# New costs in the pass that orders a transformer block's instructions: column operands, plain float32 products, result delays and load lead

## The chip, the cores and the metric

The kernel runs on one core of one Trainium2 chip. The core has a matrix engine (TensorE, PE in the profile), a vector engine (VectorE, DVE), a scalar engine (ScalarE, ACT), a general engine (GpSimd, POOL) and a queue engine (SyncE, SP) that issues nearly all DMA transfers. The metric is device time in microseconds (us) of one execution; the median of several runs is compared.

## The reference

One layer of an encoder on x of 2048 tokens by 1024 features, float32, then a last RMSNorm:

```
xn = RMSNorm(x)
aq ak av mq mk mv mo i f ga gm = split(xn @ w_in)
A = attention: own chunk of 64 and 8 chunks before, clipped relative bias, 8 heads of 64
M = mLSTM over chunks, 4 heads of 128; mq and mk pass a causal convolution of width 4 and silu;
    headwise RMSNorm, times sigmoid(mo)
y = sigmoid(ga) * (A @ w_att_proj) + sigmoid(gm) * (M @ w_mlstm_proj)
x = x + y @ w_out
x = x + relu(RMSNorm(x) @ w_up)^2 @ w_down          # w_up: 1024 x 4096
```

## The kernel before, in words

**Number format.** Each float32 operand of a large product is split into two parts, the rounded value and the rest (both of type float32r). One product is three matrix products: high by high, high by low, low by high. For a weight tile of 128x1024, ACT writes the high part (line 614) and DVE the low part (line 616) in `split_now`; for an activation tile of 128x512, lines 1324 or 1326 on ACT and 1329 or 1331 on DVE do the same in `split`. Some smaller products stay plain float32: in the recurrence (`rec_head`, lines 1786, 1800, 1801, 1802) and in sums over features.

**Stages.** The tokens are four blocks of 512. Blocks 0 and 1 are projected block by block (matmul lines 697 to 699, `mm3`), with attention and recurrence of these blocks running between. Then come products in `quad` (line 782), which forms a 2x2 block product from seven products of sums, so DVE has sums of operands and of results to make: operand sums in `take_rest` (line 1897) and `take_parts` (lines 1924, 1936), copies and sums of results in `combine` (line 1959 on ACT, line 1967 on DVE). The order is: gates and output projection of blocks 0 and 1; the projections of blocks 2 and 3 (the names in `IN_ORDER`, among them `mq` and `mk`, which go through `conv_far` with lines 2129 to 2142, and last `mo`, with lines 2100 and 2106 in `after_in`); the up and down products of blocks 0 and 1; recurrence and attention of blocks 2 and 3 between the down products; then output projection, up and down of blocks 2 and 3.

**Memory.** Nearly everything that lives long goes to DRAM and comes back: SP issues stores (line 2220) and loads (for instance 578 and 573 for weights, 1917 for inputs of the up product). Tiles come from small pools: 3 split weight tiles `wsp`, 4 raw weight tiles `wraw`, 16 tiles `ctx`, 6 `tmp`, 28 split operands `r`, 8 accumulation banks.

**What sets the order.** Two passes do. `Flow` (line 97) runs the generators and fixes the program order and which tile each step gets; the change leaves it alone. `Order` (line 226) then takes that program, finds which instruction must follow which (`graph`), and writes a fixed order for each engine, and for SP's queue, by a forward walk (`run`, line 338). Three methods feed the walk. `cost` gives each instruction a duration. `lag` gives the time from one instruction's end to the start of one that needs it. `due` gives each instruction the latest start that does not hold up the matrix products, worked back from their planned times; an SP transfer is taken there to need its own cost and `FAR` more. In the walk an engine takes, of the instructions that are ready, the one with the earliest due time; PE takes the one that is earliest in program order. When a transfer lands in the walk depends on `REACH`, `LAND` and its size, not on `FAR`.

```
for j in self.succ[k]:
    to = self.eng[j]
    r = end + self.lag(k, j)
    at[j] = max(at[j], r)
    safe[j] = max(safe[j], r + (self.MARGIN[e] if to != "PE" and (to != e or e == "SP") else 0.0))
    left[j] -= 1
    if not left[j]:
        heapq.heappush(soon[to], (safe[j], due[j], j))
```

At run time each engine goes through its list in order, and an instruction that waits holds all that stand behind it.

Of the kernel before, what the change touches and what calls it, by code (L numbers as in the profile page):

```python
# [24 lines left out]
F32 = mybir.dt.float32  # L25
# [200 lines left out]
class Order:  # L226
# [1 line left out]

    MARGIN = dict(PE=600.0, Activation=100.0, DVE=100.0, Pool=100.0, SP=2500.0)
    WAKE = dict(PE=43.0, DVE=23.0, Activation=23.0, Pool=69.0, SP=16.0)  # L230
    REACH, LAND, FAR, FLY = 1400.0, 1100.0, 2500.0, 8

    def __init__(self, tc):
        self.tc = tc
# [33 lines left out]
    def cost(self, i, e):  # L268
        ins, outs = self.operands(i.ins), self.operands(i.outs)
        n = max(self.count(a) for a in ins + outs)  # L270
        bank = any(a.tensor.name.startswith("bank") for a in ins + outs)
        if e == "PE":
            return max(110.0, 13.7 + self.count(outs[0]) / 2.4)
        if e == "SP":
            return 365.0
        if e == "Activation":
            return (75 if bank else 93) + 0.84 * n + (190 if len(outs) > 1 else 0)
        if e == "Pool":
            return 1200.0 if n <= 8 else 80 + 1.27 * n
        if n <= 4:  # L280
            return 155.0
        two = sum(self.count(a) > 4 for a in ins) > 1
        return 60 + (1.13 if two or bank else 0.66) * n + (80 if len(outs) > 1 else 0)

    def transfer(self, i):
        a, b = self.operands((i.outs[0], i.ins[0]))
# [29 lines left out]
    def lag(self, j, k):  # L316
        e, to = self.eng[j], self.eng[k]
        if e == to != "SP":
            return 0.0
        t = self.WAKE[to] + (0.0 if e == "SP" else 13.0)  # L320
        return t + (0.0 if e != "PE" else 175.0 if self.dur[j] >= 140.0 else 130.0)

    def due(self):
# [55 lines left out]
class Layer:  # L379
    LATE, LATE_SPLIT = 3000.0, 2500.0  # L380
# [2333 lines left out]
```

## Time and profile before

| | |
|---|---|
| median of 3 runs | 2759.5 us (2759.44, 2759.5, 2763.28) |
| the profiled execution | 2762.9 us, its span 2761.1 us |
| PE busy | 2748.6 us, 13054 matmuls |
| DVE busy | 2060.5 us |
| ACT busy | 1490.9 us |
| granted TensorE clock, mean | 0.999 |
| DMA | 678.64 MB, 246 GB/s |

The span is the time from the first to the last instruction; the profiled execution took 1.8 us more than its span. The busy time of PE counts matmuls that overlap in the pipeline, so PE can be busy by the profile and still issue matmuls later than it could. The time from one matmul's start to the next one's shows that better.

### The profile page before, as it was taken

What the parts mean: (1) busy time and instruction counts of PE and PEld (TensorE: products, weight loads), DVE (VectorE), ACT (ScalarE), POOL (GpSimd) and SP (SyncE); (2) the same over time, 40 slices, a digit from 0 to 9 for tenths busy, and PEclk for the clock granted to TensorE, in tenths of its full rate; (3) what the DMA queues carried; (4) which work ended last, traced back from release to release, by engine and by line L of the source; (5) the groups of instructions that cost most, each with busy time, mean ns of one, the idle gap of its engine ahead of it and who ended that gap; (6) DMA issues with size and microseconds to landing.
All of it is one profiled execution on the core that took longest, in us unless ns stands there. A gap on an engine that the chain in (4) does not pass through costs nothing.

```text
span 2761.1 us, 38681 instructions
## 1 busy us (share of the span) xinstructions
PE 2748.6 (100%) x13054; PEld 2291.3 (83%) x13054; DVE 2060.5 (75%) x3793; ACT 1490.9 (54%) x2617; POOL 49.9 (2%) x101
## 2 busy tenths in 40 slices
PE   9999999999999999999999999999999999999999
PEld 7888888888878888778888888888888888888888
DVE  7796799668996866876676788889888656555566
ACT  5664576534454545575556566566335655554444
POOL 0010001000000000000000000000000000000000
PEclk9999999999999999999999999999999999999999
DMA  7968859768866587588888978868977667676664
GB/s 283 292 220 263 235 161 305 252 199 309 279 200 228 195 285 251 170 262 311 298 288 283 303 242 253 251 203 255 293 232 262 209 218 262 237 247 215 197 222 163
DMA packets 329190, 678.64 MB, mean 246 GB/s; under 512 B 36856, under 2 KB 67744, under 8 KB 328992
## 3 DMA queue, kind: packets, MB, share of 16 engines
q1 hardware_dynamic: 328848, 676.17, 74.4%
q8 instruction: 102, 1.67, 0.3%
q14 instruction: 96, 0.79, 0.1%
q10 hardware_dynamic: 144, 0.01, 0.0%
HBM read 472.59 MB, written 203.44 MB: 245 GB/s over the span
## 4 chain that ended last, share of the span: by engine, by line
PE 95%; DVE 2%; ACT 1%; issue 1%; DMA 0%; SPq 0%; DVEq 0%; ACTq 0%
PE bank L782 42%; PE bank L697 13%; PE bank L699 13%; PE bank L698 13%; PE bank L811 3%; PE bank L1515 2%; PE bank L1488 2%; PE bank L1546 2%; PE bank L1802 1%; PE bank L1801 1%; DVE ctx L2138 1%; PE bank L1800 1%; PE bank L1786 0%; DVE wsp L616 0%; PE bank L862 0%
## 5 line engine op out<-in xcount | busy, mean ns | idle before, releaser
L782 PE MATMUL bank<-r,wsp 128*128 128x512 f32 x5544 | 1266.6, 391 | 5.4 <-ACT r L1324 2.0
L782 PEld LDWEIGHTS bank<-r,wsp 128*128 128x128 f32 x5544 | 1040.5, 188 | 223.7 <-ACT r L1324 2.5
L616 DVE TENSOR_TENSOR wsp<-wraw,wsp 128x1024 fp32r<-128x1024 f32 x458 | 560.2, 1223 | 371.1 <-ACT wsp L614 360.6
L614 ACT CAST wsp<-wraw 128x1024 fp32r<-128x1024 f32 x458 | 481.3, 1051 | 545.9 <-PE bank L698 224.4
L697 PE MATMUL bank<-r,wsp 128*128 128x512 f32 x1456 | 580.7, 399 | 0.5 <-ACT ctx L1779 0.5
L699 PE MATMUL bank<-r,wsp 128*128 128x512 f32 x1456 | 569.7, 391 | 0.0
L698 PE MATMUL bank<-r,wsp 128*128 128x512 f32 x1456 | 569.1, 391 | 0.0
L699 PEld LDWEIGHTS bank<-r,wsp 128*128 128x128 f32 x1456 | 273.6, 188 | 58.0
L697 PEld LDWEIGHTS bank<-r,wsp 128*128 128x128 f32 x1456 | 274.0, 188 | 50.9 <-ACT ctx L1779 0.9
L698 PEld LDWEIGHTS bank<-r,wsp 128*128 128x128 f32 x1456 | 274.3, 188 | 49.5
L1967 DVE TENSOR_TENSOR ctx<-bank,ctx 128x512 f32<-128x512 f32 x186 | 127.3, 688 | 103.5 <-PE bank L782 103.0
L1329 DVE TENSOR_TENSOR r<-r 128x512 fp32r<-128x512 f32 x248 | 163.4, 687 | 13.0 <-ACT r L1324 12.4
L1324 ACT CAST r<-r 128x512 fp32r<-128x512 f32 x248 | 147.5, 621 | 21.8 <-DMA r<-u 20.0
L1959 ACT COPY ctx<-bank 128x512 f32<-128x512 f32 x186 | 107.9, 581 | 81.8 <-PE bank L782 70.1
L1530 ACT ACTIVATE sc<-sc,scs 128x640 f32<-128x640 f32 (+4 forms) x128 | 97.5, 763 | 75.6 <-DVE scs L1527 69.9
L1551 DVE TENSOR_TENSOR r<-bank,r 128x512 fp32r<-128x512 f32 (+1 forms) x168 | 97.2, 597 | 20.1 <-ACT r L1549 19.1
L1549 ACT CAST r<-bank 128x512 fp32r<-128x512 f32 (+1 forms) x168 | 82.5, 518 | 51.5 <-PE bank L1546 50.0
L1521 DVE CUSTOM_DVE_ANT_0 sc<-bank,bias 128x320 f32<-128x320 f32 (+3 forms) x240 | 103.8, 463 | 3.6 <-PE bank L1515 2.8
L2298 ACT ACTIVATE ctx<-ctx 128x512 f32<-128x512 f32 x96 | 60.5, 630 | 84.8 <-DVE ctx L1967 84.7
L1488 PE MATMUL bank<-r,r 128*128 128x512 f32 x336 | 94.7, 363 | 0.0
L633 DVE TENSOR_TENSOR wraw<-wraw,wraw 128x1024 f32<-128x1024 f32 x76 | 92.8, 1223 | 1.8
L1515 PE MATMUL bank<-r,r 128*128 128x320 f32 (+3 forms) x480 | 85.7, 305 | 0.0
(269 smaller groups left out, 2738.1 us busy)
## 6 DMA issues: line engine op xcount, KB each, us to landing
wraw<-in_wf SPq DMA_DIRECT2D x178, 512.0 KB, 4.6
wraw<-wsum SPq DMA_DIRECT2D x136, 512.0 KB, 4.4
r<-u SPq DMA_DIRECT2D x224, 256.0 KB, 4.3
wraw<-in_w SPq DMA_DIRECT2D x87, 512.0 KB, 5.0
u<-ctx SPq DMA_DIRECT2D x128, 256.0 KB, 2.4
ctx<-in_wf SPq DMA_DIRECT2D x112, 256.0 KB, 4.6
wsum<-ctx SPq DMA_DIRECT2D x112, 256.0 KB, 4.5
u<-tmp SPq DMA_DIRECT2D x96, 256.0 KB, 3.7
```

What stands on the lines that cost most here:

```text
L614: nc.scalar.copy(w[:, 0], raw)
L616: nc.vector.tensor_sub(w[:, 1], raw, w[:, 0].bitcast(F32))
L697: mm(ps, lh, rh, start=first, stop=False)
L698: mm(ps, lh, rl, start=False, stop=False)
L699: mm(ps, ll, rh, start=False, stop=last)
L782: mm(ps, wv[:, x, k, n], a[:, y], start=new and k == 0 and x == y == 0, stop=k == 3 and x == 1, skip_group_check=True)
L1324: self.nc.scalar.copy(dst[:, 0], src)
L1329: self.nc.vector.tensor_sub(dst[:, 1], src, dst[:, 0].bitcast(F32))
L1488: nc.tensor.matmul(acc[:, :, c0:c0 + w], st, sl[:, :, o:o + w], start=n == 0, stop=n == total - 1)
L1515: nc.tensor.matmul(bks[x][:, :w], q[:, y, i * P:(i + 1) * P], kf[:, f * P + x * w:f * P + x * w + w], start=y == 0, stop=y == 1)
L1959: nc.scalar.copy(t[:, o:o + 512], ps)
L1967: nc.vector.tensor_add(t[:, o:o + 512], ps, t[:, o:o + 512])
```

## The change

Only `Order` is touched. What is computed, the tiles and the transfers stay as they are; the five lists can come out in another order.

- `cost`, PE: a plain float32 product counts double; transposes don't.
- `cost`, ACT: 92 ns for each input beyond the first (a column of one value per partition as scale or bias), in place of 190 ns for a second output (a sum over the row).
- `cost`, DVE: 62 ns when there are three inputs (a column among them), in place of 80 ns for a second output.
- `lag`: between instructions of one engine, where one needs the other's result, 125 ns (ACT), 85 ns (DVE) or 60 ns (POOL) in place of 0; to another engine, 98 ns more after ACT and 50 ns more after DVE.
- `FAR`: 5000 ns in place of 2500.

```diff
     WAKE = dict(PE=43.0, DVE=23.0, Activation=23.0, Pool=69.0, SP=16.0)
-    REACH, LAND, FAR, FLY = 1400.0, 1100.0, 2500.0, 8
+    AGAIN = dict(PE=0.0, Activation=125.0, DVE=85.0, Pool=60.0)
+    LATE = dict(PE=0.0, Activation=98.0, DVE=50.0, Pool=0.0)
+    REACH, LAND, FAR, FLY = 1400.0, 1100.0, 5000.0, 8
...
         if e == "PE":
-            return max(110.0, 13.7 + self.count(outs[0]) / 2.4)
+            plain = ins[0].dtype == F32 and not i.is_transpose
+            return max(110.0, 13.7 + self.count(outs[0]) / 2.4) * (2.0 if plain else 1.0)
...
         if e == "Activation":
-            return (75 if bank else 93) + 0.84 * n + (190 if len(outs) > 1 else 0)
+            return (75 if bank else 93) + 0.84 * n + 92 * (len(ins) - 1)
...
-        return 60 + (1.13 if two or bank else 0.66) * n + (80 if len(outs) > 1 else 0)
+        return 60 + (1.13 if two or bank else 0.66) * n + (62 if len(ins) > 2 else 0)
...
         if e == to != "SP":
-            return 0.0
-        t = self.WAKE[to] + (0.0 if e == "SP" else 13.0)
+            return self.AGAIN[e]
+        t = self.WAKE[to] + (0.0 if e == "SP" else 13.0 + self.LATE[e])
```

## Prediction

> **What bounds the kernel now.** I read the page first, then PE's waits, then the time from one matmul's start to the next at those waits.
>
> ```profile
> span 2761.1 us, 38681 instructions
> PE 2748.6 (100%) x13054; PEld 2291.3 (83%) x13054; DVE 2060.5 (75%) x3793; ACT 1490.9 (54%) x2617; POOL 49.9 (2%) x101
> PE 95%; DVE 2%; ACT 1%; issue 1%; DMA 0%; SPq 0%; DVEq 0%; ACTq 0%
> ```
>
> PE sets the time: 95% of the chain that ended last is matmuls. The change alters no matmul, so it can only remove PE's waits, add new ones, or change how kinds of matmuls alternate.
>
> ```profile
> PE bank L782 <- ACT r L1324: 2.0, 1, 2.0
> PE bank L782 <- ACT ctx L1959: 2.0, 1, 2.0
> PE bank L782 <- ACT r L1326: 1.1, 1, 1.1
> PE bank L438 <- DVE ones L435: 1.0, 1, 1.0
> PE bank L1645 <- DVE cum L1641: 0.7, 2, 0.3
> PE bank L697 <- ACT ctx L1779: 0.5, 1, 0.5
> PE bank L782 <- DVE r L1329: 0.2, 1, 0.2
> ```
>
> These are all of PE's named waits; L438 is the start, where nothing can be gained. The others are six places with 6.5 us of idle time. Idle time understates them, so here is PE's timeline at the three large ones.
>
> ```profile
> 715.74 1.27 PE L782 MATMUL bank<-r,wsp 128*128 128x512 f32 x4
> 718.14 0.74 PE L782 MATMUL bank<-r,wsp 128*128 128x512 f32 x2 [1.13 <-ACT r L1326]
> ...
> 1145.90 0.84 PE L782 MATMUL bank<-r,wsp 128*128 128x512 f32 x3
> 1148.74 5.30 PE L782 MATMUL bank<-r,wsp 128*128 128x512 f32 x15 [2.00 <-ACT ctx L1959]
> ...
> 1212.40 0.84 PE L782 MATMUL bank<-r,wsp 128*128 128x512 f32 x3
> 1215.28 0.50 PE L782 MATMUL bank<-r,wsp 128*128 128x512 f32 x1 [2.04 <-ACT r L1324]
> 1216.01 0.74 PE L782 MATMUL bank<-r,wsp 128*128 128x512 f32 x2 [0.23 <-DVE r L1329]
> ```
>
> Three undisturbed matmuls take 0.84, one longer than a start-to-start interval: with 0.39 for the last one the interval is (0.84 - 0.39) / 2 = 0.226 us. **C**, at 716: four intervals take 2.40 in place of 0.90, a loss of 1.5. **A**, at 1146: three take 2.84 in place of 0.68, a loss of 2.16; and the 15 matmuls behind it take 5.30 in place of 14 x 0.226 + 0.39 = 3.55, a further 1.75. **B**, at 1212: four take 3.61, a loss of 2.7. The small ones are 0.5 (**D**, L697) and 0.7 (**E**, L1645, two places); with about 0.16 hidden in the pipeline before each (0.39 - 0.226), they come to 0.7 and 1.0. The sum, 1.5 + 3.9 + 2.7 + 0.7 + 1.0 = 9.8 us, is what a perfect order could save.
>
> **What the change does, part by part.** No instruction and no byte is added: PE's 13054, DVE's 3793 and ACT's 2617 instructions and SP's transfers stay, and any of them may move in its list. The question is what the planner misjudged where PE stalled.
>
> ```profile
> 1108.00:1148.00 40.00, 38.74 (x171) 31.76 (x170) 38.26 (x55) 20.80 (x30) 0.00 (x0) 1.00 0.44 147
> L2138 DVE SCALAR_TENSOR_TENSOR ctx<-ctx,cvw,ctx 128x512 f32<-128x512 f32 x21 | 15.6, 749 | 0.6 <-ACT ctx L2131 0.2
> 1105.40 0.76 DVE ctx L2138
> 1106.18 0.75 DVE ctx L2138
> ```
>
> *Column operands and dependent steps, at A.* In the 40 us before A, DVE is busy for 38.26. The largest group is the convolution, 21 steps of L2138, each with a column and mostly needing the one before. The old formula gives 60 + 1.13 x 512 = 639 ns and no delay to the dependent one; the chain of waits has them start 0.78 us apart. The new one gives 639 + 62 + 85 = 786 ns. Over 21 steps the old plan is 21 x 0.14 = 2.9 us short, against a stall of 2.16. So PE's bank was to be emptied (L1967 on DVE, then L1959 on ACT) at a time when DVE was in truth still busy with L2138. With true durations the pass sees the queue and puts L1967 and L1959 ahead where their due times say so. They pass steps of `conv_far`, whose stores then go out later on SP; what is late next are the `ctx` tiles they free, and 16 of those exist.
>
> ```profile
> 1183.00:1214.00 31.00, 30.24 (x134) 24.73 (x132) 22.46 (x32) 24.96 (x39) 0.00 (x0) 1.00 0.84 273
> L2106 ACT ACTIVATE ctx<-ctx,ghead 128x512 f32<-128x512 f32 x8 | 6.5, 817 | 0.2
> L1924 ACT ACTIVATE ctx<-ctx,gcol 128x512 f32<-128x512 f32 x3 | 2.2, 718 | 2.7 <-DMA ctx<-x 2.7
> L1924 ACT ACTIVATE tmp<-tmp,gcol 128x512 f32<-128x512 f32 x3 | 2.1, 713 | 0.0
> 1207.29 0.33 SPq L2220
> 1207.72 6.12 DMA ctx<-x
> ```
>
> *The same at B, and the loads.* Here ACT is full until 1207. Eight L2106 with two columns and six L1924 with one cost the old plan 8 x 184 + 6 x 92 = 2.0 us less than the new one gives them. SP, which issues in order, held the load of x behind the store of the last L2106, and the load landed 6.12 us after its issue. `due` allowed 2.5 us for it.
>
> ```profile
> r<-u SPq DMA_DIRECT2D x224, 256.0 KB, 4.3
> u<-ctx SPq DMA_DIRECT2D x128, 256.0 KB, 2.4
> ```
>
> 5000 ns fits loads like r<-u (4.3 us) and overstates such stores as u<-ctx, at 2.4. In `due` this gives a step 2.5 us more urgency for each transfer between it and PE, 5 us for a store with a load behind it; the chain at B has both.
>
> [...]
>
> *Result delays and sums over a row, in attention.*
>
> ```profile
> L1530 ACT ACTIVATE sc<-sc,scs 128x640 f32<-128x640 f32 x96 | 79.7, 831 | 63.4 <-DVE scs L1527 62.8
> L1530 ACT ACTIVATION_READ_ACCUMULATOR sc<-sc,scs 128x1 f32 x128 | 24.2, 189 | 0.0
> 1540.00:1960.00 420.00, 420.00 (x2273) 360.10 (x2273) 366.19 (x955) 256.69 (x563) 12.96 (x35) 1.00 0.82 251
> ```
>
> Dropping 190 and 80 ns for a second output is wrong taken alone: L1530 still has a second instruction. The old cost of L1530 was 93 + 538 + 190 = 821, the new one 723, with 98 for its delay 821 again. L1521, 320 wide, goes by the formulas from 502 to 422, with 85 for the dependent step behind it 507. So the latencies of the softmax chain come out level or later; only ACT's occupancy is short, 128 x 98 ns = 12.5 us over stages in which ACT is busy for 256.69 of 420 us. PE does not idle there (420.00 of 420.00), since it can pass over an attention step that is not ready. I take nothing; the bound is one stall of D's size (0.7) in each of the two attention stages, 1.4, and no gain, as nothing is lost there now.
>
> *Plain products at double cost.*
>
> ```profile
> 1794.90 0.47 PE L697 MATMUL bank<-r,wsp 128*128 128x512 f32 x1
> 1795.21 0.40 PE L698 MATMUL bank<-r,wsp 128*128 128x512 f32 x1
> 1795.44 0.40 PE L699 MATMUL bank<-r,wsp 128*128 128x512 f32 x1
> 1795.68 0.39 PE L1800 MATMUL bank<-r,ctx 128*128 128x129 f32 x2
> 1795.90 0.39 PE L1801 MATMUL bank<-r,ctx 128*128 128x129 f32 x2
> L1802 PE MATMUL bank<-cst,r 128*128 128x129 f32 x128 | 24.7, 275 | 0.0
> ```
>
> Each plain product is two passes and takes 0.22 us (1795.68 to 1795.90): the new 220 ns is right, the old 110 half. The old plan thus let PE run ahead of the truth, a hidden reserve of 110 ns per product for the engines that feed it; L1802 alone has 64 products, 7 us. The reserve goes, and the added delays take its place: nothing, with the same bound of 1.4. A return from plain to split products costs 0.31 - 0.23 = 0.08 (1794.90 to 1795.21). If every fourth of L1802's 64 groups joined or left another, that is 16 x 0.08 = 1.3 either way; I take 0.
>
> **The sum.** A and B, where the planner's error is the size of the stall: 6.6, of which I take three quarters, 5.0, since DVE and ACT stay full and something else is late next. E hangs on a chain of small dependent steps, which AGAIN now prices: half, 0.5. C and D: nothing; C's work has no column, it is DVE out of time. New stalls in the reshuffled lists: one of C's size, 1.5 (between 0 and the slower rival's price). That is 5.0 + 0.5 - 1.5 = 4.0 off the profiled execution's 2762.9, 2758.9. That execution is 3.4 above the median, two of the three runs lie at 2759.5, and nothing shown says where the 3.4 is spent; I carry the difference over: 2759.5 - 4.0 = **2755.5**. Its own range is 2753 to 2758.5.
>
> [...]
>
> **The rivals.**
> 1. *All stalls go*: the six come from late planning alone and the order is now free of them: 2759.5 - 9.8 = 2749.7. For it: DVE and ACT have time left over the whole span. Against: at C DVE has none for 28 us.
> [...]
> 3. *It doesn't do what it says*: true costs change the lists little, or move a stall for each one removed: 2759.5, give or take 1.5.
> 4. *Slower: the lead starves PE's own chain.* What is stored and loaded again before use now counts as up to 5 us more urgent than what PE waits for directly. With DVE full this decides as soon as a bank's emptying is put off by more than the time until PE needs the bank, 24 matmuls or 5.4 us. At A one more convolution tile ahead of L1967 is 3 x 0.75 + 0.69 = 2.9 and the slow pace behind it 1.75; at C the five L2181, whose results are stored, would go ahead of the operand splits, 5 x 0.6 = 3.0. With no gain elsewhere: 2759.5 + 7.7 = 2767.2.
>
> ```profile
> 690.00:718.00 28.00, 27.01 (x119) 21.74 (x117) 27.74 (x44) 11.85 (x16) 0.00 (x0) 1.00 0.85 293
> L2181 DVE TENSOR_TENSOR ctx<-bank,ctx 128x512 f32<-128x512 f32 x5 | 3.4, 685 | 0.0
> ```
>
> For it: DVE is busy for 27.74 of these 28 us. Against: a `ctx` tile freed by a store is itself what L1959 needs to empty a bank.
>
> **How the numbers follow.** Chances: forecast 0.40; all stalls go 0.17; lead worthless 0.12; no effect 0.12; slower 0.19. A measurement here can tell about 0.2%, 5.5 us, from no change, so faster means below 2754.0 and slower above 2765.0. Faster: 0.17 and a third of the forecast's 0.40, 0.30. Slower: 0.19 and 0.01 of the rest, 0.20. Within: 0.50. The range runs from the first rival to just short of the fourth, 2749.5 to 2766.
>
> **What would show it.** In the changed kernel's PE waits, the rows L782 <- ACT ctx L1959 and L782 <- ACT r L1324 should be gone or under 1 us, the clock near 1150 at 1.00, and the load of x for the up product issued before the last L2106's store. L1645 <- DVE cum should shrink, L1326's row at C stay. [...] The forecast is wrong if waits named above remain and the time falls all the same: then alternation of matmul kinds or another part outside these waits matters.

## The result, and the profile after

The changed kernel's median is 2754.12 us (14 runs, 2752.87 to 2755.94), against 2760.45 us (14 runs, 2758.91 to 2765.14) for the kernel before: 6.3 us less, a ratio of 0.9976 with a 95% interval of 0.9968 to 0.9984. The forecast was 2755.5, 1.4 us above. The prediction had given faster 0.30 and no change 0.50, with a bound of 5.5 us, or 2754.0. By the difference this is just faster; by the time alone, worked from the earlier median of 2759.5, it lies 0.1 on the other side of the bound. The two profiled executions lie further apart, 2762.9 and 2753.5. Why is a point of its own below.

The page of the changed kernel, with the lines that answer to the first three shown of before (line numbers in it are 3 higher, because the change adds lines above):

```profile
span 2751.8 us, 38708 instructions
PE 2745.0 (100%) x13054; PEld 2287.2 (83%) x13054; DVE 2035.7 (74%) x3793; ACT 1491.8 (54%) x2617; POOL 51.1 (2%) x101
PE 99%; DVE 0%; DMA 0%; ACT 0%; SPq 0%; issue 0%; ACTq 0%; DVEq 0%
```

The instruction counts of PE, DVE and ACT are those of before. The chain that ended last is now matmuls for 99% in place of 95%. All of PE's named waits (what waited, on what, us in total, times, longest):

```profile
PE bank L441 <- DVE ones L438: 1.0, 1, 1.0
PE bank L785 <- DVE r L1334: 0.6, 1, 0.6
```

L441 is the start. Of the six places A to E one is left, C, and PE's timeline there and at A reads (start, length, the idle time before it in brackets):

```profile
704.73 10.34 PE L785 MATMUL bank<-r,wsp 128*128 128x512 f32 x43
715.70 2.63 PE L785 MATMUL bank<-r,wsp 128*128 128x512 f32 x10 [0.63 <-DVE r L1334]
...
1142.74 5.60 PE L785 MATMUL bank<-r,wsp 128*128 128x512 f32 x24
```

At C the last of the 43 matmuls starts at 704.73 + 10.34 - 0.39 = 714.68 and the next at 715.70, 1.02 later in place of 0.226: a loss of 0.8. But the 43 have themselves taken 10.34 in place of 42 x 0.227 + 0.39 = 9.92, and the ten behind the wait lose 0.2. In all C loses 1.4 here. Before, the same count over the 140 matmuls around it gives 1.6 (the prediction counted 1.5), so little is gained at C, although the named wait fell from 1.1 to 0.6. The 24 matmuls where A was take 5.60, which is 23 x 0.226 + 0.39: nothing is lost. The same stretches at A and B, each a little earlier than before because less was lost ahead of them (start and end, length, then busy time of PE, its weight loads, DVE, ACT, POOL, then the granted clock, DMA share and GB/s):

```profile
1108.00:1148.00 40.00, 40.00 (x178) 33.11 (x178) 37.60 (x54) 22.08 (x32) 0.00 (x0) 1.00 0.48 156
1183.00:1214.00 31.00, 31.00 (x139) 25.44 (x137) 22.28 (x33) 24.89 (x40) 0.00 (x0) 1.00 0.73 245
```

DVE is still busy for 37.60 of the 40 us at A, and ACT for 24.89 of the 31 at B. The engines that feed PE have no more time than before; their work stands in another order.

**What is different at A.** Before, DVE and ACT worked in turns, and each had put an instruction that waited for the other ahead of what PE needed. DVE's timeline before:

```profile
1146.26 0.69 DVE L2142 SCALAR_TENSOR_TENSOR ctx<-ctx,ctx 128x512 f32<-128x512 f32 x1 [0.76 <-ACT ctx L2140]
1146.86 0.68 DVE L1967 TENSOR_TENSOR ctx<-bank,ctx 128x512 f32<-128x512 f32 x1
```

ACT's timeline before, and then after:

```profile
1147.58 0.63 ACT L2100 ACTIVATE ctx<-ctx 128x512 f32<-128x512 f32 x1 [0.43 <-DVE ctx L1967]
1148.12 0.57 ACT L1959 COPY ctx<-bank 128x512 f32<-128x512 f32 x1
```

```profile
1143.07 0.57 ACT L1962 COPY ctx<-bank 128x512 f32<-128x512 f32 x1
1145.13 1.24 ACT L2103 ACTIVATE ctx<-ctx 128x512 f32<-128x512 f32 x2 [1.50 <-DVE ctx L1970]
```

These are the same copy in both lists, of bank_134 into ctx_121. Before, its row (L1959, 1148.12) names no wait of its own: it stood behind L2100, which waited 0.43 for DVE's L1967, which stood behind L2142, which waited 0.76 for ACT's L2140. PE went on at 1148.74, 0.05 after the copy's end. After, the copy (L1962) stands ahead of the waiting instruction (L2103), and the 1.50 that this one waits costs nothing. (The copy also needs its tile stored and free; whether that held before 1148.12 the rows don't say.)

**What is different at B.** ACT's timeline before, then after, then SP's after:

```profile
1210.10 1.05 ACT L614 CAST wsp<-wraw 128x1024 fp32r<-128x1024 f32 x1 [2.84 <-PE bank L782]
1213.86 0.72 ACT L1924 ACTIVATE ctx<-ctx,gcol 128x512 f32<-128x512 f32 x1 [2.70 <-DMA ctx<-x]
```

```profile
1204.14 1.05 ACT L617 CAST wsp<-wraw 128x1024 fp32r<-128x1024 f32 x1 [3.32 <-PE bank L785]
1207.57 0.73 ACT L1927 ACTIVATE ctx<-ctx,gcol 128x512 f32<-128x512 f32 x1
```

```profile
1200.14 1.02 SPq L2223 DMA_DIRECT2D mfar<-ctx  x2
1201.26 0.43 SPq L1920 DMA_DIRECT2D ctx<-x  x1
```

The weight cast is the same instruction of ACT's list in both, and PE releases it in both, so it serves as a mark: it comes 5.96 us earlier after. The load of x comes 6.46 earlier (1207.72 to 1201.26), so by that mark it gained only 0.5 us, and it still stands behind the last store that L2109 (before: L2106) feeds. The operand is ready 6.3 earlier. PE, which lost 2.7 us here, now loses nothing, because its own list changed. This is the start of the stretch in both lists (index of the matmul: output <- operands; r_88 is the split of the late tile):

```
before  5594 bank_131<-r_79  5595 bank_133<-r_88 (x3)  5598 bank_133<-r_69 (x3)  5601 bank_134<-r_88 (x3)
        5604 bank_134<-r_69 (x3)  5607 bank_131<-r_79 (x2)  5609 bank_131<-r_77 (x3)  5612 bank_131<-r_87 (x3)
after   5594 bank_131<-r_79 (x3)  5597 bank_131<-r_77 (x3)  5600 bank_131<-r_87 (x3)  5603 bank_131<-r_81
        5604 bank_133<-r_88  5605 bank_134<-r_88  5606 bank_131<-r_81  5607 bank_133<-r_88 (x2)
```

The changed walk expects the operand later and gives PE 9 other matmuls first: 9 x 0.226 = 2.0 us, the size of the idle time of before (2.04). These are the rest of bank_131, which before stood behind the late operand. With the delays alone the late operand is first used at place 5603, with the columns alone at 5592, so this move is the delays' work. In all, some 500 places of PE's list hold another matmul than before.

### The profile page after: what moved, and what is told of

Its sections match the earlier page's. It is cut to its first block, busy times and chain, and to the rows that moved or that the text cites. A ratio compares the mean times of both kernels' runs of the same rounds, so it can differ in the third digit from the quotient of the medians.

```text
span 2751.8 us, 38708 instructions
## 1 busy us (share of the span) xinstructions
PE 2745.0 (100%) x13054; PEld 2287.2 (83%) x13054; DVE 2035.7 (74%) x3793; ACT 1491.8 (54%) x2617; POOL 51.1 (2%) x101
## 4 chain that ended last, share of the span: by engine, by line
PE 99%; DVE 0%; DMA 0%; ACT 0%; SPq 0%; issue 0%; ACTq 0%; DVEq 0%
PE bank L785 45%; PE bank L700 13%; PE bank L702 13%; PE bank L701 13%; PE bank L814 3%; PE bank L1518 2%; PE bank L1491 2%; PE bank L1549 2%; PE bank L1804 1%; PE bank L1805 1%; PE bank L1789 1%; PE bank L1803 1%; PE bank L865 0%; PE bank L1592 0%; PE bank L904 0%; PE bank L1778 0%
## 5 line engine op out<-in xcount | busy, mean ns | idle before, releaser
L1962 ACT COPY ctx<-bank 128x512 f32<-128x512 f32 x186 | 107.8, 582 | 91.6 <-PE bank L785 81.2
```

What stands on the lines that cost most here:

```text
L1962: nc.scalar.copy(t[:, o:o + 512], ps)
```

## The experiments

Each is one kernel with a few lines of the ordering pass changed, compared with the kernel before on the same chip. Line numbers in a kernel shift by as many lines as its edit adds. The delays are the two tables `AGAIN` and `LATE`; the plain products are the doubled PE cost; the columns are the ACT and DVE cost lines; the lead is `FAR`. Times are medians; ratios are to the kernel before.

**A nudge.** One constant of the DVE cost of the kernel before is 1 ns larger, which says nothing new of the chip and shuffles the lists.

```diff
-        return 60 + (1.13 if two or bank else 0.66) * n + (80 if len(outs) > 1 else 0)
+        return 61 + (1.13 if two or bank else 0.66) * n + (80 if len(outs) > 1 else 0)
```

> The kernel before with one meaningless number changed: a base cost of 61 ns in place of 60 on DVE. Theory 1 (the pass was wrong about true durations at the stalls): nothing is put right, so A and B stay, PE's waits of 1 us or more keep a sum of 4 to 7 us, ratio 0.9995 to 1.0010. Theory 2 (a redraw: any new order happens to have other stalls, and the order before was an unlucky one): most of the gain appears here too, ratio 0.9975 to 0.9985, and the stalls lie elsewhere.

2759.54 us, ratio 0.9994 (0.9985 to 1.0003), profiled execution 2758.68. PE's waits:

```profile
PE bank L782 <- ACT ctx L1959: 1.7, 1, 1.7
PE bank L782 <- ACT r L1326: 1.1, 1, 1.1
PE bank L782 <- ACT r L1324: 0.8, 1, 0.8
```

PE's timeline at A:

```profile
1139.76 6.51 PE L782 MATMUL bank<-r,wsp 128*128 128x512 f32 x28
1147.95 10.27 PE L782 MATMUL bank<-r,wsp 128*128 128x512 f32 x44 [1.68 <-ACT ctx L1959]
```

A, B and C stall in the same places with the same releasers: a new draw of the lists alone doesn't take them away. Their size moves, though: the waits of 1 us or more come to 2.8 us, where 4 to 7 was expected. A loses 1.9 (1139.76 + 27 x 0.226 = 1145.86 to 1147.95, less 0.226), and no slow pace follows: 44 matmuls in 10.27 are 43 x 0.23 + 0.39. B waits 0.8 in place of 2.0.

**The lead alone**, in the kernel before.

```diff
-    REACH, LAND, FAR, FLY = 1400.0, 1100.0, 2500.0, 8
+    REACH, LAND, FAR, FLY = 1400.0, 1100.0, 5000.0, 8
```

> The kernel before with the lead for loads at 5000 ns alone. Theory 1 with the lead as one of its causes: B goes (the load of x for the up product is issued some us earlier), A and the other waits stay, 2.5 to 3 us, ratio 0.9988 to 0.9992. The slower rival (the lead starves PE's own chain): A grows by 2 us or more and C grows, ratio above 1.0005. Theory 2: like the nudge.

2758.32 us, ratio 0.9988 (0.998 to 0.9997), profiled execution 2757.74. Of its PE waits:

```profile
PE bank L782 <- ACT ctx L1959: 1.3, 1, 1.3
PE bank L1800 <- DMA r<-mvfar: 1.1, 1, 1.1
...
PE bank L782 <- DVE r L1331: 0.2, 1, 0.2
```

B is gone, and here it is the lead that removes it: SP issues the load of x at 1201.76, 6 us earlier, and PE's list uses the late operand 10 matmuls sooner than before (place 5585), without a wait. A shrinks, C's wait is down to 0.2, E stays, and a load of `mvfar` is late that was not. Nothing of the kind that the slower rival named appears: no new stall behind DVE steps whose results are stored.

**The columns alone**, with the second-output terms dropped as in the change, in the kernel before.

```diff
-            return (75 if bank else 93) + 0.84 * n + (190 if len(outs) > 1 else 0)
+            return (75 if bank else 93) + 0.84 * n + 92 * (len(ins) - 1)
...
-        return 60 + (1.13 if two or bank else 0.66) * n + (80 if len(outs) > 1 else 0)
+        return 60 + (1.13 if two or bank else 0.66) * n + (62 if len(ins) > 2 else 0)
```

> The kernel before with the new costs of column operands (ACT 92 ns each, DVE 62 ns) in place of the second-output costs, alone. Theory 1: A shrinks by about half (1.3 of the 2.9 us by which the plan was short there) and B by 2 us of planning, so 2 to 4 us off, ratio 0.9986 to 0.9993. If the dropped second-output cost hurts, new small waits behind the softmax steps, lines 1530 to 1551, 0.3 to 1.4 us. Theory 2: like the nudge.

2757.18 us, ratio 0.9986 (0.9977 to 0.9995), profiled execution 2758.08.

```profile
PE bank L782 <- ACT r L1326: 1.1, 1, 1.1
...
PE bank L1645 <- DVE cum L1641: 0.6, 2, 0.3
PE bank L699 <- DVE r L1282: 0.5, 1, 0.5
```

A and B are gone with the columns alone; C and E stay whole, as steps without a column should. D's row has given way to one of the same size at L699; a fourth wait, of 0.2, is at L1546.

**The delays alone**, in the kernel before.

```diff
+    AGAIN = dict(PE=0.0, Activation=125.0, DVE=85.0, Pool=60.0)
+    LATE = dict(PE=0.0, Activation=98.0, DVE=50.0, Pool=0.0)
...
-            return 0.0
-        t = self.WAKE[to] + (0.0 if e == "SP" else 13.0)
+            return self.AGAIN[e]
+        t = self.WAKE[to] + (0.0 if e == "SP" else 13.0 + self.LATE[e])
```

> The kernel before with the result delays alone (AGAIN within an engine, LATE to another). Theory 1: A shrinks by the other half (1.6 us of planning error is the dependent steps' delay) and the two waits at the gates' running maximum, E, go; B stays unless the delays reach it; 2 to 4 us off, ratio 0.9986 to 0.9993. Theory 2: like the nudge.

2762.96 us, ratio 1.0009 (1.0 to 1.0017), profiled execution 2766.78: no gain. PE's waits:

```profile
PE bank L1225 <- POOL r_far L1257: 3.4, 1, 3.4
PE bank L1802 <- DMA r<-mvfar: 3.3, 1, 3.3
...
PE bank L784 <- DVE r L1333: 0.4, 1, 0.4
```

The load that ends the second, in the chain of waits of that stretch (issued, time to landing):

```profile
442.92 9.99 DMA r<-mvfar
```

PE's timeline behind the first (3.44 us in it), and the stretch there with the columns of above:

```profile
502.12 0.63 PE L700 MATMUL bank<-r,wsp 128*128 128x512 f32 x1
502.55 0.63 PE L701 MATMUL bank<-r,wsp 128*128 128x512 f32 x1
```

```profile
501.80:504.50 2.70, 2.70 (x8) 2.12 (x8) 1.29 (x2) 1.92 (x5) 0.00 (x0) 0.50 0.00 1
```

A, B and E are gone here too, and C (L784) waits 0.4. But two stalls of 3.3 and 3.4 us have come, both in the recurrence and its norm, where PE works on plain products. The walk of this kernel prices those at half (110 ns, where the prediction's rows have 0.22 us), so in it PE arrives there, and everything else is planned, at times that are not the chip's. How much of the two stalls is due to that, and how much to a load and a power that took long in this execution, it doesn't separate. They are hardly this execution's alone: all 11 executions of this kernel have a mean granted clock of 0.999 or less on record. Here it is 0.998, most likely for what lies behind the two stalls: a clock of 0.50 behind the first, and behind the second plain products that start 0.42 to 0.44 us apart in place of 0.22.

**Each part taken back from the changed kernel.** Four kernels, each the changed one without one part: `FAR` at 2500; the plain products at single cost; the old ACT and DVE cost lines; no delays (the diffs above, backwards, and for the plain products this):

```diff
-            return max(110.0, 13.7 + self.count(outs[0]) / 2.4) * (2.0 if plain else 1.0)
+            return max(110.0, 13.7 + self.count(outs[0]) / 2.4)
```

Without the lead:

> The changed kernel with the lead for loads back at 2500 ns. Theory 1 (the true durations and delays remove the stalls, the lead adds little since columns alone and delays alone each removed B without it): ratio to before 0.9972 to 0.9984, no wait of 1 us or more. Theory 3 (the lead is what keeps the load of the recurrence's values, r<-mvfar, ahead, which came 3.4 us late with the delays alone): that wait of 1 to 4 us at the third recurrence product is back, ratio 0.9985 to 1.0005.

2753.44 us, ratio 0.9974 (0.9964 to 0.9984); one wait, the one at C, of 0.4. The lead adds nothing to the other parts, and the late operand of B is used at place 5604, exactly as in the changed kernel.

Without the plain products' cost:

> The changed kernel with plain float32 products at single cost again. Theory 1: the same as the changed kernel within 0.0005, the removed reserve costs nothing. Theory 4 (the two late places of the delays-alone kernel, near 449 and 498 us, come from PE running ahead in the plan, since recurrence products take 110 ns each too little there): the waits at the recurrence's load and at the row of r_far are back, 2 to 7 us in all, ratio 0.9985 to 1.0010.

2757.02 us, ratio 0.9987 (0.9978 to 0.9996).

```profile
PE bank L1778 <- DMA r<-mfar: 0.8, 1, 0.8
...
PE bank L1226 <- POOL r_far L1258: 0.7, 1, 0.7
```

A load for the recurrence and POOL's L1258 are late again, the kind of wait that the delays alone had brought, though smaller. The part is worth about 3 us, 0.9987 against 0.9976. The two intervals overlap, but the times of this kernel (2755.45 to 2760.02) and of the one without the lead on the same chip (2753.14 to 2754.60) don't.

Without the columns:

> The changed kernel with the old costs of columns and second outputs. Theory 1 with two causes that each suffice: A stays away through the delays and B through the lead or the delays, so within 0.0005 of the changed kernel. If columns are needed: A is back with 1 to 2 us, ratio to before 0.9980 to 0.9990.

2754.87 us, ratio 0.9979 (0.997 to 0.9988); again one wait, at C, of 0.7. A and B do not come back as waits: the delays remove them as well. The starts of PE's matmuls still show something at B: 131 matmuls from 1194.82 on take 30.56, 0.7 more than 130 x 0.227 + 0.39 = 29.9, where the changed kernel loses under 0.1.

Without the delays:

> The changed kernel without the result delays. Theory 1: A and B stay away (columns alone removed both), but E, the waits at the gates' running maximum, 0.3 us each by the idle time, are back, and C is as large as in the columns-alone kernel unless the lead shrinks it: 1 to 2.5 us slower than the changed kernel, ratio to before 0.9980 to 0.9990. If the delays do the most: A or B back, ratio above 0.9990.

2759.75 us, ratio 0.9997 (0.9988 to 1.0005). The longest of its waits:

```profile
PE bank L1648 <- DVE cum L1644: 0.6, 2, 0.3
PE bank L1491 <- DVE r L1554: 0.5, 1, 0.5
```

No large stall is left, but eleven small ones are there, in ten rows, nearly all of them at lines of attention and recurrence and of the projections between which these run. With the 0.16 us hidden ahead of each they come to 5.1, where the one wait of the changed kernel comes to 0.8; the span is 5.3 above that of the changed kernel, the median 5.6. The time expected was 1 to 2.5 above. Nearly the whole gain is gone. This is the part that the change can't do without.

**The plain products alone**, in the kernel before.

```diff
+            plain = ins[0].dtype == F32 and not i.is_transpose
+            return max(110.0, 13.7 + self.count(outs[0]) / 2.4) * (2.0 if plain else 1.0)
```

> The kernel before with plain float32 products at double cost alone. If the halved cost was a reserve that hid the missing delays (the removed-reserve argument of the prediction): A and B stay as before and new small waits of 0.2 to 0.6 us appear in the attention and recurrence stages, as in the kernel without delays; ratio 0.9995 to 1.0015. If the halved cost only did harm: some of the small waits (D) go and nothing new comes, ratio 0.9985 to 0.9998.

2761.72 us, ratio 1.0005 (0.9996 to 1.0014), profiled execution 2761.37. PE's timeline at A, and the stretch behind it:

```profile
1150.28 3.01 PE L783 MATMUL bank<-r,wsp 128*128 128x512 f32 x12 [1.98 <-ACT ctx L1960]
```

```profile
1152.00:1154.00 2.00, 2.00 (x10) 1.69 (x9) 0.82 (x2) 1.53 (x2) 0.00 (x0) 1.00 0.87 119
```

A and C stay, B is down to two waits of 0.2 (its operand is used at place 5595, as before), and small waits for ACT come, up to 0.4. By itself this part gains nothing.

**Delays and plain products together**, in the kernel before, without columns and lead (the two diffs above).

> The kernel before with the result delays and the doubled plain products, without the new column costs and without the lead. If these two carry the change (each of the four kernels with one part left out says so): no wait of 1 us or more, the late load of the recurrence's values and the late row of r_far of the delays-alone kernel gone, ratio to before 0.9973 to 0.9983. If the columns or the lead are needed as a second cover: A or B back at 1 to 2 us, ratio 0.9983 to 0.9992.

2755.91 us, ratio 0.9982 (0.9973 to 0.9991). The largest wait:

```profile
PE bank L1803 <- DVE wsp L619: 0.6, 1, 0.6
```

One part alone gives 1.0009, the other 1.0005, both 0.9982: in the kernel before neither is of use without the other. Of the 3.4-us stalls none is left.

**Fewer changes between kinds of matmul.** The changed kernel, with one rule more in the walk: a plain product or transpose that is ready waits up to 1500 ns while split products are ready, and then all that are ready go together.

```diff
+    HOLD = 1500.0
...
-                k = heapq.heappop(soon[e])[2]
+                s, _, k = heapq.heappop(soon[e])
+                if e == "PE" and kind[k]:
+                    came[k] = s + hold[k]
+                    heapq.heappush(held, (k, k))
+                    continue
...
+            now = e == "PE" and held and (last or not ripe[e] or min(came[x] for x, _ in held) <= t)
+            k = heapq.heappop(held if now else ripe[e])[1]
```

> The changed kernel with one rule more in the forward walk: on PE a plain float32 product or transpose that becomes ready waits up to 1500 ns while split products are ready, and once one runs all that are ready follow, so that PE changes from plain to split products less often (some 200 times by the written order in place of some 300). If each such return costs 0.08 to 0.09 us, as the prediction read it from the timeline: 8 to 9 us less than the changed kernel, ratio to before 0.994 to 0.996, as long as attention and recurrence don't run late. If the return's price is covered by something else: ratio as the changed kernel, 0.997 to 0.9985. If the held steps come too late for the stages behind: new waits, above 0.9985.

2760.22 us, ratio 0.9998 (0.999 to 1.0007): 6.1 us slower than the changed kernel, although the trace counts 213 returns from plain to split products in place of 258. What a return costs is seen in the kernel before, at a place where only the last plain product and the first split one are out of step:

```profile
1792.04 0.39 PE L1802 MATMUL bank<-cst,r 128*128 128x129 f32 x2
1792.18 0.48 PE L697 MATMUL bank<-r,wsp 128*128 128x512 f32 x1
1792.49 0.40 PE L698 MATMUL bank<-r,wsp 128*128 128x512 f32 x1
```

The first split matmul takes 0.31 to the next start in place of 0.23, as the prediction said, but the plain product ahead of it (two passes) has taken 0.14 in place of 0.22. Together it is 0.45 in either case: a return costs about 0.01 us, not 0.08, and there was nothing to save. What the rule cost instead is known in part. The two largest of PE's waits:

```profile
PE bank L1815 <- DMA r<-mvfar: 0.7, 1, 0.7
PE bank L797 <- DVE r L1346: 0.7, 1, 0.7
```

With two more, of 0.5 and 0.3, they come to 2.2 us in place of 0.6. Place by place in PE's list, this execution is 3.1 us behind that of the changed kernel at 480 us, 2.7 of it from 390 us on, where the recurrence runs and the waits of 0.7 (for `mvfar`) and 0.3 stand. By 1960 us it is 0.8 further behind, the last matmuls add 1.3, and 1.4 more pass behind the last one: together the 6.6 us by which the span grew (2758.4 against 2751.8). What else than the named waits made PE late there stays open.

**A price for sums over a row put back.** The changed kernel, with 92 ns on ACT and 70 ns on DVE for a second output, which the change had dropped.

```diff
-            return (75 if bank else 93) + 0.84 * n + 92 * (len(ins) - 1)
+            return (75 if bank else 93) + 0.84 * n + 92 * (len(ins) - 1) + (92 if len(outs) > 1 else 0)
...
-        return 60 + (1.13 if two or bank else 0.66) * n + (62 if len(ins) > 2 else 0)
+        return 60 + (1.13 if two or bank else 0.66) * n + (62 if len(ins) > 2 else 0) + (70 if len(outs) > 1 else 0)
```

> The changed kernel with a cost for the second output put back beside the new ones (92 ns on ACT, 70 ns on DVE), so that softmax and row sums are no longer counted too short. If the dropped cost is covered by the delays, as the prediction argued: within 0.0005 of the changed kernel, ratio to before 0.9970 to 0.9981, and no new waits. If it did harm that the changed kernel hides elsewhere: up to 1 us faster, the 0.8 us at the operand sums near 715 remaining either way. If the lists react to any change (the redraw theory): waits of 1 us or more in new places, ratio 0.998 to 1.000.

2755.98 us, ratio 0.9983 (0.9974 to 0.9992): outside what was expected, but not told apart from the changed kernel; its profile has the wait at C and two of 0.5 us for loads of the recurrence. Dropping the term cost nothing that can be told.

## Why the prediction was right or wrong

**The places and the mechanism: right.** The stalls came from a plan whose durations were off, and they went when the durations were mended; a shuffle doesn't do it. The nudge moves some 180 places of PE's list, the lead alone and the plain products alone some 300 each, and A stays in all three. As foreseen, the rows L782 <- ACT ctx L1959 and L782 <- ACT r L1324 are gone, E shrank, the clock near 1150 is at 1.00 (from 1150 to 1155 us), and a wait at C stayed (now on DVE's low part, L1334, in place of ACT's high part). In the profile the first rival came true in nearly every part: A, B, D and E are gone, 3.9 + 2.7 + 0.7 + 1.0, and C gave 0.2, so 8.5 of the 9.8 us, where the spans differ by 9.3. Yet the time is within 1.4 us of the forecast. That is luck: two steps of the sum were off, in opposite directions.

**"Three quarters", "half", "nothing" for D, and 1.5 us of new stalls: each too cautious.** The sum counted on 4.0 us where 8.5 went. The reason given, that DVE and ACT stay full and something else is late next, does not hold. They stay as full as they were (37.60 of 40 us at A), but at A and B nothing was late for want of time. At A the copy stood behind an instruction that waited, and at B PE stood before an operand that its own list could have put off by 2.0 us. A wait that comes from order can go altogether, without an engine being any freer. C, where I had said that DVE is out of time, could have shrunk too. By the starts of PE's matmuls it loses 1.6 before, 0.5 with the lead alone, 0.8 with the delays alone, 1.7 with the columns. Only lead and delays together have it back at 1.4; without the lead the whole change has it at 0.8. So "nothing" for C came out nearly right in the whole change, but not because DVE has no time. The new stalls, which did come with single parts (3.3 and 3.4 us with the delays alone), are absent from the whole change.

**"I carry the difference over": this step failed.** The profiled execution of before lay 3.4 above the median then shown, and the prediction took its 9.8 us as every run's. Place by place in PE's list, that execution falls 9.4 us behind the profiled one of the changed kernel: 3.9 at A, 2.9 at B, 1.7 ahead of C, 0.2 at C and 0.6 elsewhere. The nudge's execution, at 2758.7, falls only 5.1 behind it: by this count A costs it 2.0, with no slow pace behind, and B 1.0. So 3.9 of the 4.2 us by which these two executions differ lie in the very stalls that the prediction measured. This rests on the nudge's list, which is nearly but not wholly that of before; no second profile of before was taken.

The clocks on record point the same way for A. One stretch of 3.41 us at half clock brings the mean over 2761 us to 0.9994, recorded as 0.999. Of the 106 executions of before that ran beside the experiments, 61 have 0.999 or less, and on each chip their median time is 0.8 to 2.1 us above that of the rest. In the eight kernels whose profiles have A and B gone and a mean clock of 1.0, 8 of 89 executions have it. (The kernel with the holding rule has it in all 11, also with A and B gone, so a mean of 0.999 can come without them.) So the slow pace behind A, 1.75 us, most likely comes in about half of the executions of before. The mean doesn't say where the clock was low, so this is argued, not shown. The medians fell by 6.3, less than the 9.3 of the two profiles.

**Columns at A and B: right in cause, and not the only cover.** Columns alone remove both stalls, delays alone remove both. So the working by column costs (2.9 us short against a stall of 2.16) was a sufficient account and not the one that decides in the full change, where leaving the columns out costs nothing that these times can tell (0.9979 against 0.9976), and by the starts of PE's matmuls 0.7 us at B.

**The lead: credited in vain.** The step gave it B's late load. Alone it does remove B, by an earlier load. In the whole change the load still stands behind the last L2106's store, where I had said that it would pass it, and by the mark of the weight cast it gains only 0.5 us; B goes by the order of PE's own matmuls, and without the lead the time is the same (0.9974), with C 0.6 shorter. So beside the other parts the lead is worth nothing, for which the prediction's chance was 0.12, and B goes without it. Short transfers are not the reason: in this row of the changed kernel 256 KB land in 4.4 us at the median, nearer to the 5.0 of the new `FAR` than to the 2.5 of the old.

```profile
r<-u SPq DMA_DIRECT2D x224, 256.0 KB, 4.4
```

**Plain products at double cost: "nothing" was wrong.** The working said that a hidden reserve goes and that the delays replace it. That holds: without the delays the changed kernel, doubling included, has ten rows of small waits. What was missed is the other half. With the delays in and the cost still single, the plan has PE ahead of the chip in the recurrence, and its loads and POOL's part of the norm come too late (waits of 0.8 and 0.7); the doubling is then worth 0.9987 - 0.9976 = 0.0011, about 3 us, and with the delays by themselves 1.0009 - 0.9982 = 0.0027, about 7. The bound of 1.4 was too small in either case.

**Result delays, and sums over a row.** The delays were priced as a latency in the softmax chain that comes out level, with no gain to be had, bound 1.4. Taken back, they cost 5.6 us: without them the reserve is gone and nothing stands in its place. That PE can pass over an attention step which isn't ready holds for the walk alone; at run time its list is fixed, and it waits. Beside the columns the two parts were taken as nothing together; from the columns alone (0.9986) to the whole change (0.9976) it is about 2.8 us, in which the named waits fall from 2.4 to 0.6 (E, L699 and part of the wait at C), though the two intervals overlap. Sums over a row were rightly taken as nothing.

**Alternation.** The price of 0.08 us was wrong, the true one is about 0.01 (0.45 us in either case, from 1792.04 on); it stood in the sum with 0, so no harm came of it.

**The slower rival fell.** With the lead alone, where it should have been at its worst, A lost less (a wait of 1.3), C lost less, and the one new wait of 1 us or more was for a load of `mvfar`, not behind DVE steps whose results are stored.

**The clock behind a stall.** The slow pace after A in the profile of before is the clock. It is still at 1.00 for the first 1.41 us behind the stall, then at 0.50 for 3.41 us, then back at full speed. Behind B it is at 1.00 (same columns as the stretches above, three at A and one at B):

```profile
1148.74:1150.15 1.41, 1.41 (x6) 1.19 (x7) 1.38 (x3) 0.00 (x0) 0.00 (x0) 1.00 0.91 334
1150.15:1153.56 3.41, 3.41 (x10) 2.67 (x9) 0.93 (x2) 1.53 (x2) 0.00 (x0) 0.50 0.80 213
1153.56:1154.00 0.44, 0.44 (x3) 0.36 (x3) 0.44 (x2) 0.33 (x2) 0.00 (x0) 0.99 1.02 391
1215.00:1222.00 7.00, 6.49 (x27) 4.98 (x28) 6.67 (x10) 5.89 (x11) 0.00 (x0) 1.00 0.40 131
```

The stall of 2.00 at A has half clock behind it, the one of 2.04 at B has not. With the plain products alone the stall of 1.98 at A has a clock of 1.00 behind it (the stretch from 1152 shown there), and behind the nudge's 1.68 the matmuls keep their pace of 0.23. With the delays alone the stall of 3.4 has a clock of 0.50 behind it (the stretch from 501.80, matmuls 0.43 apart), and the pace behind the one of 3.3 is half as well. So the 1.75 us that the prediction put to A do not come from the size of a stall alone. What else decides it no run here shows.

## What to carry to other kernels

When a planner's order stalls an engine, look first for an instruction that stands behind one that waits, or for other work that the engine had ready; such a stall can go entirely although the engines around it are as full as before. Mend a planner's times together: each of two right corrections (delays, plain products) made this kernel no faster alone, and the two together gave most of the gain, because one wrong price had been hiding another. Other single corrections can each give part of it: the columns alone and the lead alone came to 0.9986 and 0.9988. And before a stall in one profiled execution is taken as every run's, compare that execution's time and mean clock with those of the others: the difference may lie in that very stall.

## What was not expected of the hardware

POOL's power of 128x4 elements, the releaser of the 3.4-us stall with the delays alone, took four times as long there as in the kernel before (and 2.58 us without the plain products' cost, where PE waited 0.7 for it). POOL's timeline before, then with the delays alone:

```profile
495.43 1.38 POOL L1255 TENSOR_TENSOR r_far<-r_far,half 128x4 f32<-128x4 f32 x1 [15.95 <-DVE r_far L1253]
```

```profile
495.95 5.52 POOL L1257 TENSOR_TENSOR r_far<-r_far,half 128x4 f32<-128x4 f32 x1 [11.67 <-DVE r_far L1255]
```

DVE was busy beside the power in both, with four splits of L1329 before (2.54 us from 495.25) and five adds of L1899 then (3.09 us from 495.78), so a busy DVE alone doesn't account for it; whether the adds do was not tried, and the cause stays open. The load of `mvfar` that took 9.99 us, where the 16 such loads land in 6.0 at the median in the kernel before (at most 6.2) and in 5.9 in the changed one (at most 8.7), is as unexplained.
